# A transformer block with 32 routed experts: another order in the front, and a routing transition that keeps its second half off GpSimd

## The chip, the core and the metric

The kernel runs on one core of a Trainium2 chip. A core has five engines with a queue of instructions each: TensorE (PE; its weight loads are listed as PEld), VectorE (DVE), ScalarE (ACT), GpSimd (POOL) and SyncE (SP, which here only issues DMA transfers). An engine runs its queue in order; semaphores make an instruction wait for those of other engines. The metric is device time in microseconds, the median of several runs; chances further down are meant against the median before.

## What is computed

One layer on x (1024 tokens of 1024 numbers), float32, cut to what matters:

```python
c_act = silu(c)
sh1, sc1, gt1, sh2, sc2, gt2 = split(c_act @ w_ada + b_ada, 6)
h = rms_norm(x, g_mix) * (1 + sc1) + sh1
q_lat, kv_lat, k_rope, q_b, k_b, v_b, gate_a, gate_b = split(h @ w_in)
x = x + gt1 * (sigmoid(gate_a) * (mla(...) @ w_oa) + sigmoid(gate_b) * (band(...) @ w_ob)) @ w_out
h = rms_norm(x, g_ffn) * (1 + sc2) + sh2
group = top 1 of softmax(h @ w_rg + b_rg)               # 4 groups
two experts = top 2 of softmax((h @ w_re + b_re)[group]) # 8 in each group
x = x + gt2 * sum over the two of weight * (silu(h @ w_gate[e]) * (h @ w_up[e])) @ w_down[e]
return rms_norm(x, g_final)
```

## The kernel before

The program is recorded through a scheduler, which fixes each engine's order when it is built; `tc.issue_after(i)` tells it not to place instructions before i. Tiles come from shared pools of fixed places: `t8` (8 KB a partition, 18 places), `t4` (4 KB, 10) and `t2` (6). A transfer into a place waits until its former tile has been read for the last time. Products need more than one rounded factor: a float32 operand is split into a high part (ScalarE, L67 or L380) and a rest (VectorE, L68 or L381), and one product becomes three TensorE instructions (L72 to L74).

**The front** (`front`, L301). x comes in eight tiles of 128 tokens, four to a half, with the modulation weights `wada` (eight of 1 MB) and the latent weights `wl` (two of 832 KB). SP issues the first half of x, wada 0, wl 0, wada 1, the second half of x, wada 2, wl 1 (L324 to L333). For each half, `normal` (L345) squares the four tiles on ScalarE into one scratch place `junk` (L349), takes the reciprocal root in eleven small VectorE steps (L82 to L91) and scales the tiles (L352). `turn` (L357) transposes them, 32 TensorE instructions a half (L361), and ScalarE copies the result to `xT` (L362). `shift_scale(k)` (L367) makes the 128 shifts and 128 scales of block k of eight by two sums over a wada tile on VectorE (L371), `modulate` (L375) applies them on ScalarE (L378) and splits the result. `latent(h, k, pl)` adds the block's 12 products for half h. For the first four blocks the halves go apart (`APART = 4`), after that together. Values (L72 with `wvh`) follow directly; behind them come projections and attention to about 868 us.

**The merge and the routing** (`merge` L1000, `route` L1147, the class at L1547). Eight tiles of tokens get their output projection (L72 to L74 into `pp`), `gt1` times it (L1568, `part`), the sum with x (L1569), a sum of squares on ScalarE (L1577), the reciprocal root, and then the second modulation: a VectorE step x·rstd·a2 (L1594) and a GpSimd addition of sh2 (L1595), whose result is stored for the experts to gather. Logits come from x before its modulation (L1614; the scale is folded into `wr`), and `route(first, n)` takes them for four, two and two tiles: logits times rstd plus bias (L1157, L1158), the two largest of each group (L931 to L941), a mask of chosen experts `M` (L1177, L1178), running counts on TensorE (L1184, L1185), each token's place (`A`, L1212), and with these the list of tokens of each expert `idx` (L1238) and the weights `comb` (L1252). After the last call GpSimd gathers the tokens of expert 0 (L1341) and TensorE transposes them (L1492).

**The experts** (`weights`, L1277). 96 weights of 1 MB flow through a ring: the first 17 have places of their own (`RAW + RAW4`), 15 as one tile and two as pairs of 512 KB; later ones go round 14 whole places (`RAW2`) and the two pairs. From the fourth on a load waits for the last but one (L1299).

Of the kernel before, what the change touches and what calls it, by code (L numbers as in the profile page):

```python
# [19 lines left out]
P = 128  # L20
# [39 lines left out]
class Kernel:  # L60
# [240 lines left out]
    def front(self, c):  # L301
# [33 lines left out]
        load_mod(0)  # L335
        load_lat(0)
        load_mod(1)
        load_x(1)
# [5 lines left out]

        def normal(h):  # L345
            hs = slice(4 * h, 4 * h + 4)
            for t in range(4 * h, 4 * h + 4):
                junk = self.t4([P, D], F32, "junk")
                nc.scalar.activation(junk, xs[t], AF.Square, accum_out=ss[:, t:t + 1])  # L349
# [7 lines left out]
        def turn(h):  # L357
            for k in range(KD):
# [8 lines left out]
        def shift_scale(k):  # L367

            w = mods.pop(k)
            for i, (to, b) in enumerate(((shc, 19), (scc, 27))):  # L370
                nc.vector.tensor_tensor_reduce(w[:, i], w[:, i], cb, op0=OP.mult, op1=OP.add, scale=0.5,  # L371
                                               scalar=cols[:, b + k:b + k + 1], accum_out=to[:, k:k + 1])
            nc.vector.tensor_scalar(scc[:, k:k + 1], scc[:, k:k + 1], 1.0, cols[:, 8 + k:9 + k], op0=OP.add, op1=OP.mult)

        def modulate(k, *halves):  # L375
            cs = slice(halves[0] * HALF, (halves[-1] + 1) * HALF)
            y = self.H(xt, k)[:, cs]
            last = nc.scalar.activation(y, y, AF.Identity, bias=shc[:, k:k + 1], scale=scc[:, k:k + 1])  # L378
            hi = self.H(hh, k)[:, cs]
# [3 lines left out]
        hh, hl = ([self.t8([P, 2, S], F32R, nm) for _ in range(4)] for nm in ("hh", "hl"))  # L383
        self.hh, self.hl = hh, hl
        lat = [self.t8([P, 4, LAT], F32, "lat") for _ in range(2)]
# [9 lines left out]
        def keep(pl, h):  # L395
            for t in range(4):
                nc.scalar.copy(lat[h][:, t], pl[t])
# [47 lines left out]
        rooted = normal(0)  # L445
        turn(0)
# [3 lines left out]

        def begin(k):
            load_mod(k + 3)
            shift_scale(k)
            self.split(wlh[k // 4][:, k % 4], wll[k // 4][:, k % 4], wl[k // 4][:, k % 4])
        for k in range(APART):
            with tc.issue_after(rooted.ins):
                begin(k)
            parted[k] = modulate(k, 0)[1]
            latent(0, k, pl)
            if k == 1:  # L460
                rooted = normal(1)
                turn(1)
        nxt += [self.bank()[:, 0:LAT] for _ in range(4)]
        for k in range(APART):
            modulate(k, 1)
            latent(1, k, nxt)
        for k in range(APART, KD):
            with tc.issue_after(parted[max(k - 3, 0)].ins):
                begin(k)
# [453 lines left out]
    def first_max(self, rw, src, rows, n, name):  # L923

        nc = self.nc

        def wide(t):
            return t.rearrange("p (a o) -> p a o", o=1).to_broadcast([P, rows, n])
        iom = self.iom[:, 0:n].rearrange("p (o e) -> p o e", o=1).to_broadcast([P, rows, n])
        m = rw.tile([P, rows], F32, name=name + "m")  # L930
        nc.vector.tensor_reduce(m, src, op=OP.max, axis=AX.X)  # L931
        yield
        t = rw.tile([P, rows, n], F32, name=name + "t")
# [4 lines left out]
        f = rw.tile([P, rows], F32, name=name + "f")  # L938
# [61 lines left out]
    def merge(self):  # L1000
# [43 lines left out]
        self.X = [self.t4([P, D], F32, "X") for _ in range(2)]  # L1044
# [4 lines left out]
        for u in range(4):  # L1049
            steps = second.project(u, 1)  # L1050
            for _ in range(TURN_AT):
                next(steps)
            if u > 0:
                turn(second, u - 1)
            next(route, None)
            if u == 2:
                most = self.route(4, 2)
                next(most)
            elif u == 3:
                next(most)  # L1060
# [11 lines left out]
        next(most)  # L1072
        route = self.route(6, 2)
# [3 lines left out]
        stored = second.modulate(3)  # L1077
# [69 lines left out]
    def route(self, first, n):  # L1147
# [4 lines left out]
        lg = rw.tile([P, n, 4], F32, name="lg" + tag)  # L1152
        le = rw.tile([P, 4 * n, 8], F32, name="le" + tag)
        u = self.rstd[:, hs].rearrange("p (a o) -> p a o", o=1)
        for to, cs in ((le.rearrange("p (a g) e -> p a (g e)", a=n), slice(4, 36)), (lg, slice(0, 4))):
            w = cs.stop - cs.start
            nc.vector.tensor_mul(to, self.logits[first - base][:, base:base + n, cs], u.to_broadcast([P, n, w]))  # L1157
            nc.vector.tensor_add(to, to, self.rbias[:, cs].rearrange("p (o e) -> p o e", o=1).to_broadcast([P, n, w]))  # L1158
        found = {}

        def groups():
            found["g"] = yield from self.first_max(rw, lg, n, 4, "g" + tag)

        def tops():
            found["a"] = yield from self.first_max(rw, le, 4 * n, 8, "a" + tag)
# [3 lines left out]
            found["b"] = yield from self.first_max(rw, le, 4 * n, 8, "b" + tag)  # L1169
# [4 lines left out]
        mine = goh.rearrange("p a (g o) -> p (a g) o", o=1).to_broadcast([P, 4 * n, 8])  # L1174
        M = rw.tile([P, n, E], BF16, name="M" + tag)
        flat = M.rearrange("p a (g e) -> p (a g) e", g=4)
# [10 lines left out]
        for j, o in enumerate((oh1, oh2)):  # L1187
            nc.vector.tensor_mul(oh[:, :, j].rearrange("p a (g e) -> p a g e", g=4),
                                 o.rearrange("p (a g) e -> p a g e", a=n),
                                 goh.rearrange("p a (g o) -> p a g o", o=1).to_broadcast([P, n, 4, 8]))  # L1190
# [7 lines left out]
        nc.gpsimd.tensor_mul(m2, m2, goh.rearrange("p a g -> p (a g)"))  # L1198
        nc.vector.tensor_reduce(d[:, :, 4], m2.rearrange("p (a g) -> p a g", a=n), op=OP.add, axis=AX.X)
# [24 lines left out]
        C = self.t2([P, 2 * n, 3, E], BF16, "C")  # L1224
        nc.gpsimd.tensor_mul(C, oh8.rearrange("p n (o e) -> p n o e", o=1).to_broadcast([P, 2 * n, 3, E]),
                             parts.rearrange("p n (c o) -> p n c o", o=1).to_broadcast([P, 2 * n, 3, E]))
# [12 lines left out]
        yield  # L1239
        for i in range(N):  # L1240
# [36 lines left out]
    def weights(self, n):  # L1277

        for _ in range(n):
# [6 lines left out]
            elif j < RAW + RAW4:  # L1286
                w = [self.t4([P, D], F32, "we4") if j == RAW or c == 0 else self.more.tile([P, D], F32, name="we_more")
# [47 lines left out]

    def experts(self):
# [3 lines left out]
        def gather(e):  # L1340
            nc.gpsimd.indirect_dma_start(  # L1341
                out=X[e % 2], out_offset=None, in_=self.scratch["h2"],
                in_offset=bass.IndirectOffsetOnAxis(ap=self.idx[:, e:e + 1], axis=0),
                bounds_check=S - 1, oob_is_err=False)
# [4 lines left out]
        gather(0)  # L1349
        gather(1)  # L1350
        self.weights(RAW4 - 1)
# [192 lines left out]
class Mix:  # L1544
# [27 lines left out]
    def square(self, u, cs):  # L1572
# [4 lines left out]
        k.nc.scalar.activation(self.h2[u][:, cs], self.x1[u][:, cs], AF.Square, accum_out=ss)  # L1577
# [11 lines left out]
    def modulate(self, u):  # L1589
# [4 lines left out]
        nc.vector.scalar_tensor_tensor(h2, self.x1[u], k.rstd[:, t:t + 1], k.a2, op0=OP.mult, op1=OP.mult)  # L1594
        nc.gpsimd.tensor_add(h2, h2, k.sh2)  # L1595
# [26 lines left out]
def lay_out(i):  # L1622
# [6 lines left out]
    def col(v):  # L1629
# [16 lines left out]
        "w_mod": f["w_ada"][0][:, 0:2 * D].T.reshape(2, KD, P, D).transpose(1, 2, 0, 3),  # L1646
# [19 lines left out]
    }  # L1666
    return {k: np.ascontiguousarray(v) for k, v in out.items()}
# [16 lines left out]
```

## Time and profile before

| | us |
|---|---|
| median of 3 runs | 1294.43 |
| lowest, highest | 1293.18, 1301.65 |
| profiled execution | 1290.75 |
| its span | 1289.0 |
| PE busy | 1170.5 (91%) |
| DVE busy | 846.8 (66%) |
| ACT busy | 647.2 (50%) |
| POOL busy | 375.8 (29%) |

The profile is of one execution. Its span runs from the first to the last record; 1.75 us lie around it. Busy shares are means over stages that differ: TensorE works nearly without a break in most of the span, and stands for longer stretches in the first 45 us, around the routing at 870 to 906 us, and after 1244 us.

### The profile page before, as it was taken

Reading aid. Unit: us, or ns where it says so; the run is one execution under the profiler, and the core shown is the slowest. Engines: PE = TensorE matmul, PEld = TensorE weight load, DVE = VectorE, ACT = ScalarE, POOL = GpSimd, SP = SyncE. Lnnn points to the kernel's source line nnn. Section 1 sums busy time; section 2 is a strip of 40 time slices with the busy share of each in tenths; the row PEclk is TensorE's granted clock in tenths of the full one; section 3 lists DMA queues with packets and bytes.
Section 4 is the critical chain, followed back from the end, with each engine's and each line's share of the span. In section 5 each row is a group of like instructions: output and inputs, shape, how many; then the busy total and the mean of one; then the engine's idle time right before and its main releaser. Section 6 shows DMA issues by size and latency. Waiting matters only on the chain.

```text
span 1289.0 us, 17451 instructions
## 1 busy us (share of the span) xinstructions
PE 1170.5 (91%) x5802; PEld 941.2 (73%) x5802; DVE 846.8 (66%) x1709; ACT 647.2 (50%) x1277; POOL 375.8 (29%) x429
## 2 busy tenths in 40 slices
PE   3899989999999999999799999995899999998970
PEld 2887878788888888888688888874677667665640
DVE  6864636766766444677798826658777778666644
ACT  5563443544545445556678713212656656554522
POOL 0010322322322222233346465324223223232210
PEclk8999999999999999999899999996899999999985
DMA  9325885355453344797755455966788899989957
GB/s 377 133 95 190 249 262 177 112 166 186 127 183 112 99 135 140 265 317 230 210 182 161 160 201 172 366 246 244 243 289 287 294 312 295 311 308 299 313 172 272
DMA packets 102612, 286.50 MB, mean 222 GB/s; under 512 B 16453, under 2 KB 35013, under 8 KB 88344
## 3 DMA queue, kind: packets, MB, share of 16 engines
q1 hardware_dynamic: 84600, 242.34, 54.6%
q0 software_dynamic: 10864, 26.24, 8.1%
q10 hardware_dynamic: 7056, 16.78, 3.6%
q8 instruction: 47, 0.77, 0.2%
q14 instruction: 45, 0.37, 0.1%
HBM read 233.90 MB, written 68.17 MB: 234 GB/s over the span
## 4 chain that ended last, share of the span: by engine, by line
PE 59%; DMA 23%; DVE 9%; ACT 5%; issue 3%; POOL 1%; SPq 0%; DVEq 0%; POOLq 0%; ACTq 0%
DMA scratch_x<-eo,idx 11%; PE bank L72 9%; PE bank L74 9%; PE bank L73 9%; PE pp L74 4%; PE pp L72 4%; PE pp L73 4%; PE pp L1537 4%; DMA X<-scratch_h,idx 3%; PE bank L573 3%; PE bank L585 2%; PE bank L584 2%; DMA w<-in_w_g 2%; DMA scratch_oa<-ohl 2%; PE pp L1492 1%
## 5 line engine op out<-in xcount | busy, mean ns | idle before, releaser
L68 DVE TENSOR_TENSOR whl<-we,whl 128x1024 fp32r<-128x1024 f32 x125 | 150.3, 1221 | 52.4 <-ACT whl L67 49.2
L67 ACT CAST whl<-we 128x1024 fp32r<-128x1024 f32 x125 | 129.3, 1054 | 71.3 <-PE pp L74 55.3
L558 POOL TENSOR_SCALAR pr<-pr,total 128x640 f32<-128x640 f32 (+7 forms) x128 | 96.5, 756 | 209.3 <-DVE total L557 174.0
L72 PE MATMUL bank<-hh,wx 128*128 128x512 f32 x384 | 154.6, 402 | 1.4 <-DVE pl L68 1.4
L73 PE MATMUL bank<-hl,wx 128*128 128x512 f32 x384 | 151.4, 394 | 0.0
L74 PE MATMUL bank<-hh,wx 128*128 128x512 f32 x384 | 151.2, 395 | 0.0
L556 ACT ACTIVATE pr<-st,lowest 128x640 f32<-128x640 f32 (+7 forms) x128 | 89.7, 702 | 68.5 <-DVE lowest L549 43.1
L1398 POOL DMA_INDIRECT scratch_x<-eo,idx x32 | 55.9, 1747 | 229.0 <-DMA scratch_x<-eo,idx 87.8
L1537 PE MATMUL pp<-we,hT 128*128 128x512 f32 x248 | 115.6, 608 | 3.6 <-DMA we<-in_w_e 2.7
L72 PE MATMUL pp<-whl,xh 128*128 128x512 f32 x256 | 112.9, 441 | 3.5 <-ACT whl L67 3.4
L73 PE MATMUL pp<-whl,xh 128*128 128x512 f32 x256 | 104.4, 408 | 3.2 <-DVE whl L68 3.2
L68 DVE TENSOR_TENSOR pl<-bank,ph 128x512 fp32r<-128x512 f32 (+1 forms) x152 | 91.0, 612 | 23.0 <-ACT ph L67 21.1
L74 PE MATMUL pp<-whl,xl 128*128 128x512 f32 x256 | 101.4, 396 | 0.0
L592 POOL TENSOR_TENSOR ohl<-o,ohl 64x256 fp32r<-64x256 f32 x64 | 52.0, 813 | 138.2 <-ACT ohl L591 95.6
L67 ACT CAST ph<-bank 128x512 fp32r<-128x512 f32 (+1 forms) x152 | 77.6, 530 | 27.4 <-PE bank L573 25.4
L573 PE MATMUL bank<-ident,pr 128*128 128x128 f32 x528 | 81.8, 276 | 6.8 <-DVE st L553 6.7
L1537 PEld LDWEIGHTS pp<-we,hT 128*128 128x128 f32 x248 | 47.0, 194 | 52.0 <-issue 44.0
L72 PEld LDWEIGHTS bank<-hh,wx 128*128 128x128 f32 x384 | 72.7, 189 | 16.7 <-issue 2.6
L74 PEld LDWEIGHTS bank<-hh,wx 128*128 128x128 f32 x384 | 72.6, 189 | 15.3
L73 PEld LDWEIGHTS bank<-hl,wx 128*128 128x128 f32 x384 | 72.6, 189 | 12.4
L573 PEld LDWEIGHTS bank<-ident,pr 128*128 128x128 f32 x528 | 60.8, 141 | 12.7 <-issue 6.9
L73 PEld LDWEIGHTS pp<-whl,xh 128*128 128x128 f32 x256 | 48.7, 190 | 20.7 <-DVE whl L68 8.1
(375 smaller groups left out, 2820.3 us busy)
## 6 DMA issues: line engine op xcount, KB each, us to landing
we<-in_w_e SPq DMA_DIRECT2D x85, 1024.0 KB
mw<-in_w_ada SPq DMA_DIRECT2D x64, 256.0 KB
we<-in_w_e SPq DMA_DIRECT2D x17, 512.0 KB
x<-in_x SPq DMA_DIRECT2D x16, 512.0 KB
wada<-in_w_mod SPq DMA_DIRECT2D x8, 1024.0 KB
w<-in_w_g SPq DMA_DIRECT2D x16, 512.0 KB
scratch_gate<-gs ACTq DMA_DIRECT2D x32, 256.0 KB
gt<-scratch_gate SPq DMA_DIRECT2D x32, 256.0 KB
```

The costliest lines, as they stand in the source:

```text
L67: nc.scalar.copy(hi, src)
L68: (eng or nc.vector).tensor_sub(lo, src, hi.bitcast(F32))
L72: mm(ps, lh, rh, start=start, stop=False)
L73: mm(ps, lh, rl, start=False, stop=False)
L74: mm(ps, ll, rh, start=False, stop=stop)
L556: nc.scalar.activation(pv, sv, AF.Exp, bias=lowest, scale=-1.0, accum_out=total)
L558: nc.gpsimd.tensor_scalar(pr[:, 0:w], pr[:, 0:w], total, 1.0, op0=OP.mult, op1=OP.mult)
L573: nc.tensor.transpose(tp[:, i * P:(i + 1) * P], probs[s][:, lc:lc + P], self.ident)
L584: nc.tensor.matmul(o, vt[:, kb], pt["h"][:, src:src + n * P], start=i == 0, stop=False)
L592: nc.gpsimd.tensor_sub(hl[rows, 1], o[rows], hl[rows, 0].bitcast(F32))
L1398: self.nc.gpsimd.indirect_dma_start(out=self.scratch["x1"], out_offset=bass.IndirectOffsetOnAxis(ap=rows, axis=0), in_=o, in_offset=None, ...
L1537: nc.tensor.matmul(po[n], hT[:, ks], w[:, ns], start=k == 0, stop=k == 1)
```

## The change

In the front:

- x's second half is loaded right behind wada 0, ahead of wl 0 and wada 1.
- The squares (`sums`) of tiles 1 and 3 of the first half are made on VectorE (`SQUARES`), the others on ScalarE as before; all still write the one free `junk` place.
- For block 0 (`DIRECT = 1`) the scale comes from eight TensorE products with one column (L381 of the changed file) and one addition, in place of one of the two VectorE sums; the host lays out that part of wada 0 for it.
- The first transposes of half 0 are followed by its first modulation, and the other transposes come after; the second half's squares, scaling and transposes follow directly on block 0's products. `APART` is 2.

At the routing:

- For the second half of the tiles x·a2 is multiplied on VectorE right at the square (which now writes a scratch tile), and one VectorE step multiplies by rstd and adds sh2; GpSimd's addition is gone there.
- The logits of a tile are scaled and get their bias in one VectorE step a tile.
- The recorded order of `merge` differs: the last tile's modulation and store come ahead of the third call of `route`; the gathers of experts 0 and 1 are recorded before the last part of `route`; the product `C` is placed later.
- The ring: `RAW` 14, `RAW2` 13, `RAW4` 3, so three of the 16 round places are pairs; X takes one t8 tile. `LATE` is 3.

```diff
-LATE = 4
+LATE = 3
-APART = 4
+APART, DIRECT, SQUARES = 2, 1, ((1, 3), ())
-SPLIT, RAW, RAW2, RAW4 = 4, 15, 14, 2
+SPLIT, RAW, RAW2, RAW4 = 4, 14, 13, 3
         load_x(0)
         load_mod(0)
+        load_x(1)
         load_lat(0)
         load_mod(1)
-        load_x(1)
...
+        def sums(h):
+            for t in range(4 * h, 4 * h + 4):
+                junk = self.t4([P, D], F32, "junk")
+                if t % 4 in SQUARES[h]:
+                    nc.vector.tensor_tensor_reduce(junk, xs[t], xs[t], op0=OP.mult, op1=OP.add, scale=1.0, scalar=0.0,
+                                                   accum_out=ss[:, t:t + 1])
+                else:
+                    nc.scalar.activation(junk, xs[t], AF.Square, accum_out=ss[:, t:t + 1])
...
+            if k < DIRECT:
+                wk = w[:, 1].rearrange("p (b c) -> p b c", b=KD)
+                pc = self.bank()
+                for r in range(KD):
+                    nc.tensor.matmul(pc[:, 0:1], wk[:, r], cact[:, r:r + 1], start=r == 0, stop=r == KD - 1)
+                nc.vector.tensor_add(scc[:, k:k + 1], pc[:, 0:1], cols[:, 27 + k:28 + k])
...
-        rooted = normal(0)
-        turn(0)
+        sums(0)
+        normal(0)
+        weights(0)
+        turn(0, range(1))
+        modulate(0, 0)
+        turn(0, range(1, KD))
...
             latent(0, k, pl)
-            if k == 1:
+            if k == 0:
+                sums(1)
                 rooted = normal(1)
                 turn(1)
...
-        for to, cs in ((le.rearrange("p (a g) e -> p a (g e)", a=n), slice(4, 36)), (lg, slice(0, 4))):
-            w = cs.stop - cs.start
-            nc.vector.tensor_mul(to, self.logits[first - base][:, base:base + n, cs], u.to_broadcast([P, n, w]))
-            nc.vector.tensor_add(to, to, self.rbias[:, cs].rearrange("p (o e) -> p o e", o=1).to_broadcast([P, n, w]))
+        for i in range(n):
+            nc.vector.scalar_tensor_tensor(lr[:, i], self.logits[first - base][:, base + i], self.rstd[:, first + i:first + i + 1],
+                                           self.rbias, op0=OP.mult, op1=OP.add)
...
+        if self.half:
+            k.nc.vector.tensor_mul(self.h2[u][:, cs], self.x1[u][:, cs], k.a2[:, cs])
...
-        nc.vector.scalar_tensor_tensor(h2, self.x1[u], k.rstd[:, t:t + 1], k.a2, op0=OP.mult, op1=OP.mult)
-        nc.gpsimd.tensor_add(h2, h2, k.sh2)
+        if self.half:
+            nc.vector.scalar_tensor_tensor(h2, h2, k.rstd[:, t:t + 1], k.sh2, op0=OP.mult, op1=OP.add)
+        else:
+            nc.vector.scalar_tensor_tensor(h2, self.x1[u], k.rstd[:, t:t + 1], k.a2, op0=OP.mult, op1=OP.mult)
+            nc.gpsimd.tensor_add(h2, h2, k.sh2)
```

What this makes of the engines' queues is seen at three places. Line numbers in a row are those of the file that it comes from. First TensorE's queue where the second half's transposes (L361, in the changed file L367) stand against the first latent products (`st<-wlh,hh`: half 0; `bank<-wlh,hh`: half 1); before:

```order
L73 MATMUL st<-wll,hh 128x416
L74 MATMUL st<-wlh,hl 128x416
L361 MATMUL bank<-ident,x 128x128 x32
L72 MATMUL bank<-wlh,hh 128x416
L73 MATMUL bank<-wll,hh 128x416
```

and now:

```order
L381 MATMUL bank<-cact,wada 128x1 x8
L367 MATMUL bank<-ident,x 128x128 x41
L72 MATMUL st<-wlh,hh 128x416 x2
L367 MATMUL bank<-ident,x 128x128 x19
L73 MATMUL st<-wll,hh 128x416
L74 MATMUL st<-wlh,hl 128x416
L72 MATMUL st<-wlh,hh 128x416
```

All 64 transposes but four now stand ahead of the third latent product; before, 24 products of half 0 stood between the two halves' transposes.

Second, ScalarE's queue from the squares to the first modulation (L378, now L392); before:

```order
L349 ACTIVATE junk,ss<-x 128x1024 x4
L362 COPY xT<-bank 128x512 x2
L349 ACTIVATE junk,ss<-x 128x1024
L362 COPY xT<-bank 128x512 x3
L349 ACTIVATE junk,ss<-x 128x1024
L362 COPY xT<-bank 128x512 x2
L67 CAST wlh<-wl 128x416 x2
L349 ACTIVATE junk,ss<-x 128x1024
L67 CAST wlh<-wl 128x416 x2
L362 COPY xT<-bank 128x512
L378 ACTIVATE xT<-xT,shc,scc 128x512 x2
L349 ACTIVATE junk,ss<-x 128x1024
```

and now:

```order
L352 ACTIVATE junk,ss<-x 128x1024
L317 ACTIVATE cb<-st 128x1024
L352 ACTIVATE junk,ss<-x 128x1024 x5
L368 COPY xT<-bank 128x512 x2
L392 ACTIVATE xT<-xT,shc,scc 128x512
L397 CAST hh<-xT 128x512
L368 COPY xT<-bank 128x512 x5
L67 CAST wlh<-wl 128x416 x4
L368 COPY xT<-bank 128x512 x4
```

The second half's four squares stood between copies, casts and modulations; now all of them come before the first copy.

Third, VectorE's queue at the routing, where the last tile's `part` and sum with x stand against the second call of `route` (names with 0; `M_8919` is its mask); before:

```order
L1178 TENSOR_TENSOR M_8919<-M_8919,g0t 128x64
L1208 RECIPROCAL den_9007<-den_9007 128x4
L1181 TENSOR_TENSOR before<-before,M_8919 128x32
L1210 SCALAR_TENSOR_TENSOR vals<-den_9007 128x2
L1181 TENSOR_TENSOR before<-before,M_8919 128x32
L1202 TENSOR_TENSOR slot_at<-oh,pp 128x128
L1206 TENSOR_REDUCE place<-slot_at 128x4
L1212 TENSOR_TENSOR A<-io,place 128x512
L1568 TENSOR_TENSOR part<-pp,gt_7757 128x512
L1569 TENSOR_TENSOR x_8484<-x_8484,part 128x512
```

and now:

```order
L966 TENSOR_TENSOR b0t<-lr_8891,b0m 128x64
L968 TENSOR_TENSOR b0t<-b0t,iom 128x64
L1606 TENSOR_TENSOR part<-pp,gt_7760 128x512
L971 TENSOR_REDUCE b0f<-b0t 128x8
L1233 TENSOR_REDUCE d_9066<-b0m 128x2
L1607 TENSOR_TENSOR x_8487<-x_8487,part 128x512
L973 TENSOR_TENSOR b0t<-iom,b0f 128x64
L1238 TENSOR_REDUCE den_9074<-d_9066 128x2
L1241 TENSOR_SCALAR den_9074<-d_9066 128x2
L1618 TENSOR_TENSOR h_8999<-x_8487,a_7862 128x512
L1212 TENSOR_TENSOR M_8919<-a0t,b0t 128x64
L1223 TENSOR_TENSOR oh<-b0t,g0t 128x2x32
```

The last tile's sum with x moved from behind the whole second call to the middle of it, ahead of its mask, and the two kinds of work now alternate.

## Rows read from the trace of the kernel before

**Rows 1.** Stretches: length; PE, PEld, DVE, ACT, POOL busy (instructions); PE's clock; DMA; GB/s
```profile
0.00:30.30 30.30, 10.58 (x36) 6.98 (x36) 18.63 (x69) 18.82 (x35) 0.70 (x6) 0.91 0.93 375
30.30:44.70 14.40, 10.82 (x57) 9.87 (x57) 13.80 (x33) 6.47 (x13) 0.00 (x0) 0.83 0.50 208
44.70:78.00 33.30, 33.30 (x169) 32.86 (x169) 18.54 (x30) 19.14 (x28) 0.00 (x0) 0.95 0.20 64
78.00:868.00 790.00, 764.00 (x4083) 646.44 (x4082) 497.77 (x1120) 391.33 (x885) 265.11 (x332) 0.99 0.59 193
882.90:905.90 23.00, 8.02 (x44) 6.48 (x44) 20.00 (x61) 6.60 (x11) 12.72 (x24) 0.50 0.47 156
```
**Rows 2.** ScalarE's order of time, 6 to 38 us: start, duration, line, operation, idle before
```profile
18.48 1.07 ACT L362 COPY xT<-bank 128x512 f32<-128x512 f32 x2 [6.15 <-PE bank L361]
28.59 1.09 ACT L349 ACTIVATE junk<-x 128x1024 f32<-128x1024 f32 x1
```
**Rows 3.** VectorE's order of time, 6 to 38 us
```profile
12.35 0.17 DVE L82 TENSOR_SCALAR rs_v<-ss 128x4 f32<-128x4 f32 x1 [1.69 <-ACT junk L349]
14.53 2.74 DVE L352 TENSOR_SCALAR x<-x,rstd 128x1024 f32<-128x1024 f32 x4
17.19 1.28 DVE L371 CUSTOM_DVE_ANT_0 wada<-wada,cb,cols 128x1024 f32<-128x1024 f32 x1
24.52 1.09 DVE L68 TENSOR_TENSOR wll<-wl,wlh 128x416 fp32r<-128x416 f32 x2 [2.17 <-ACT wlh L67]
32.96 2.74 DVE L352 TENSOR_SCALAR x<-x,rstd 128x1024 f32<-128x1024 f32 x4
```
**Rows 4.** TensorE's order of time, 0 to 45 us
```profile
15.43 6.91 PE L361 MATMUL bank<-ident,x 128*128 128x128 f32 x32 [8.75 <-DVE x L352]
30.33 0.72 PE L72 MATMUL st<-wlh,hh 128*128 128x416 f32 x1 [7.99 <-ACT hh L380]
36.91 0.35 PE L74 MATMUL st<-wlh,hl 128*128 128x416 f32 x1
37.10 1.91 PE L361 MATMUL bank<-ident,x 128*128 128x128 f32 x16
44.68 0.46 PE L72 MATMUL bank<-wlh,hh 128*128 128x416 f32 x1 [3.20 <-ACT hh L380]
```
**Rows 5.** Shorter stretches of TensorE alone: us, PE busy (x), PEclk, DMA share, GB/s
```profile
15.40:17.10 1.70, 1.67 (x8) 1.00 0.99 395
21.40:22.20 0.80, 0.80 (x8) 1.00 0.96 399
30.30:35.10 4.80, 4.77 (x14) 0.50 1.00 416
```
**Rows 6.** VectorE's order of time at the routing, 868 to 906 us
```profile
876.95 2.33 DVE L1158 TENSOR_TENSOR lg<-lg,rbias 128x8 f32<-128x8 f32 x1
...
885.40 0.68 DVE L1568 TENSOR_TENSOR part<-pp,gt 128x512 f32<-128x512 f32 x1
886.12 0.69 DVE L1569 TENSOR_TENSOR x<-x,part 128x512 f32<-128x512 f32 x1
...
891.13 2.38 DVE L1158 TENSOR_TENSOR le<-le,rbias 128x64 f32<-128x64 f32 x1
893.44 0.15 DVE L1158 TENSOR_TENSOR lg<-lg,rbias 128x8 f32<-128x8 f32 x1
893.55 0.22 DVE L931 TENSOR_REDUCE a2m<-le 128x8 f32<-128x64 f32 x1
...
899.84 0.80 DVE L1238 TENSOR_TENSOR idx<-slot_acc 128x32 int32<-128x32 f32 x1
```
**Rows 7.** GpSimd's order of time there
```profile
891.10 2.34 POOL L1595 TENSOR_TENSOR h<-h,sh 128x1024 f32<-128x1024 f32 x1 [4.93 <-ACT whl L67]
```
**Rows 8.** TensorE's order of time there: the last tile's last projection product; expert 0
```profile
877.45 0.40 PE L74 MATMUL pp<-woh,m 128*128 128x512 f32 x1
...
905.92 1.30 PE L1492 MATMUL pp<-ident,X 128*128 128x128 f32 x5 [4.80 <-DMA X<-scratch_h,idx]
```
**Rows 9.** SP's waits, 905 to 1260 us: total, times, longest
```profile
SPq L1299 <- DMA we<-in_w_e: 251.9, 68, 8.6
SPq L1299 <- DMA we_more<-in_w_e: 18.2, 5, 5.9
SPq L1299 <- DVE comb L1252: 11.8, 1, 11.8
```

More of the change, by code (lines that the diff above doesn't have):

```diff
@@ L355, in front, with turn @@
         xt = [self.t8([P, 2, S], F32, "xT") for _ in range(4)]
-        def turn(h):
-            for k in range(KD):
+        def turn(h, ks=range(KD)):
+            for k in ks:
                 pt = self.bank()
@@ L381, in modulate @@
             return last, nc.vector.tensor_sub(self.H(hl, k)[:, cs], y, hi.bitcast(F32))
-        hh, hl = ([self.t8([P, 2, S], F32R, nm) for _ in range(4)] for nm in ("hh", "hl"))
+        hh, hl = [], []
         self.hh, self.hl = hh, hl
-        lat = [self.t8([P, 4, LAT], F32, "lat") for _ in range(2)]
+        lat = {}
         ssl = one.tile([P, NT, 2], F32, name="ssl")
@@ L449, in front @@
         nxt, parted = [], {}
[L451 to L454, printed above, removed]
         for k in range(APART):
-            with tc.issue_after(rooted.ins):
-                begin(k)
-            parted[k] = modulate(k, 0)[1]
+            if k > 0:
+                weights(k)
+            if k > 0:
+                modulate(k, 0)
+            split_lat(k)
             latent(0, k, pl)
-            if k == 1:
+            if k == 0:
+                sums(1)
                 rooted = normal(1)
@@ L464, in front @@
         for k in range(APART):
-            modulate(k, 1)
+            parted[k] = modulate(k, 1)[1]
             latent(1, k, nxt)
         for k in range(APART, KD):
-            with tc.issue_after(parted[max(k - 3, 0)].ins):
-                begin(k)
+            with tc.issue_after(parted[k - 3].ins if k > 2 else rooted.ins):
+                weights(k)
+                split_lat(k)
             last, parted[k] = modulate(k, 0, 1)
@@ L937, in first_max @@
         yield
-        f = rw.tile([P, rows], F32, name=name + "f")
+        f = rw.tile([P] + rows, F32, name=name + "f")
         nc.vector.tensor_reduce(f, t, op=OP.min, axis=AX.X)
@@ L1043, in merge @@
         project(second, 3, 0)
-        self.X = [self.t4([P, D], F32, "X") for _ in range(2)]
+        both = self.t8([P, 2, D], F32, "X")
+        self.X = [both[:, i] for i in range(2)]
         for x in self.X:
@@ L1072, in merge @@
         next(most)
+        next(most)
+        stored = second.modulate(3)
         route = self.route(6, 2)
@@ L1076, in merge @@
             pass
-        stored = second.modulate(3)
+        next(route)
+        next(route)
+        for e in range(2):
+            self.gather(e)
         for _ in route:
@@ L1168, in tops @@
             yield
-            found["b"] = yield from self.first_max(rw, le, 4 * n, 8, "b" + tag)
+            found["b"] = yield from self.first_max(rw, le, [n, 4], 8, "b" + tag)
         chains = [tops(), groups()]
@@ L1239, in route @@
         yield
+        C = self.t2([P, 2 * n, 3, E], BF16, "C")
+        with ExitStack() as c:
+            if first == 6:
+                c.enter_context(self.tc.issue_after(self.routed.ins))
+            nc.gpsimd.tensor_mul(C, oh8.rearrange("p n (o e) -> p n o e", o=1).to_broadcast([P, 2 * n, 3, E]),
+                                 parts.rearrange("p n (c o) -> p n c o", o=1).to_broadcast([P, 2 * n, 3, E]))
         for i in range(N):
@@ L1286, in weights @@
             elif j < RAW + RAW4:
-                w = [self.t4([P, D], F32, "we4") if j == RAW or c == 0 else self.more.tile([P, D], F32, name="we_more")
+                w = [self.t4([P, D], F32, "we4") if j < RAW + RAW4 - 1 or c == 0 else self.more.tile([P, D], F32, name="we_more")
                      for c in range(2)]
@@ L1334, in halves, with gather @@
         return wh, wl
+    def gather(self, e):
+        self.nc.gpsimd.indirect_dma_start(
+            out=self.X[e % 2], out_offset=None, in_=self.scratch["h2"],
+            in_offset=bass.IndirectOffsetOnAxis(ap=self.idx[:, e:e + 1], axis=0),
+            bounds_check=S - 1, oob_is_err=False)
     def experts(self):
@@ L1338, in experts @@
         X = self.X
[L1340 to L1344, printed above, removed]
+        gather = self.gather
         def scatter(e, o):
             self.add_rows(o, self.idx[:, e:e + 1])
-        gather(0)
-        gather(1)
-        self.weights(RAW4 - 1)
+        self.weights(RAW + RAW4 - len(self.loads))
         self.xT = [self.t4([P, KD, P], F32R, nm) for nm in ("xh", "xl")]
@@ L1576, in square @@
         ss = k.small.tile([P, 1], F32, name="ss%d" % cs.start)
-        k.nc.scalar.activation(self.h2[u][:, cs], self.x1[u][:, cs], AF.Square, accum_out=ss)
+        out = k.t2([P, D], BF16, "squares") if self.half else self.h2[u]
+        k.nc.scalar.activation(out[:, cs], self.x1[u][:, cs], AF.Square, accum_out=ss)
+        if self.half:
+            k.nc.vector.tensor_mul(self.h2[u][:, cs], self.x1[u][:, cs], k.a2[:, cs])
         return ss
@@ L1645, in lay_out @@
         "c_row": f["c"].reshape(1, D),
-        "w_mod": f["w_ada"][0][:, 0:2 * D].T.reshape(2, KD, P, D).transpose(1, 2, 0, 3),
+        "w_mod": f["w_ada"][0][:, 0:2 * D].T.reshape(2, KD, P, D).transpose(1, 2, 0, 3).copy(),
         "w_ada": f["w_ada"][0][:, 2 * D:],
@@ L1666, in lay_out @@
     }
+    out["w_mod"][0:DIRECT, :, 1] = (f["w_ada"][0][:, D:2 * D].reshape(KD, P, KD, P)
+                                    .transpose(2, 1, 0, 3).reshape(KD, P, D)[0:DIRECT])
     return {k: np.ascontiguousarray(v) for k, v in out.items()}
```

54 lines of the change are left out of this document (30 added, 24 removed).

## The prediction

> **What bounds the kernel now.** I began with a table of stretches. From 78 to 868 us TensorE is busy 764.0 of 790 us, and from 44.7 to 78.0 all 33.3 [rows 1]. Nothing the change touches lies there, and a packed stretch keeps its length when it starts earlier. What can be won is idle TensorE time: 19.7 us in the first 30.3, 3.6 in the next 14.4, 15.0 of the 23 us around the routing [rows 1]. So I read the order of time of TensorE in these stretches, then of the engines it waits for.
>
> In the front TensorE transposes at 15.43, then waits 8.0 us for `hh`, makes 24 products, transposes the second half at 37.10 and waits 3.2 us again before 44.68 [rows 4]. The second half is late because its squares stand between copies on ScalarE: the last begins at 28.59 [rows 2], the reciprocal root and the scaling (2.74 from 32.96) follow [rows 3]. At the routing the last projection product ends at 877.85 [rows 8], but `part` reads it at 885.40 [rows 6]: VectorE has the whole second call of `route` ahead of it. Twice a tiny addition there takes 2.3 to 2.4 us, where another of its kind takes 0.15 [rows 6]; the second runs with GpSimd's addition of sh2 from 891.10 to 893.44 [rows 7]. Expert 0 waits for `idx` and its gather until 905.92 [rows 6, 8]. Last I read SP's waits: after the routing it waits mostly for weights, and once, 11.8 us, for `comb`, the routing's last result [rows 9].
>
> **The front, step by step.** Moving x ahead of 1.9 MB: x, wada 0 and nothing else are 5.2 MB, 14 us at the 375 GB/s of the first 30 us [rows 1], a mean that includes the empty start; I take 14 to 17 us for x's last tile. With no copies between them, the second half's squares (1.09 each) end about 1.2 us later, at 18; before, the last ended at 29.7 [rows 2]. VectorE's two squares in the first half win little: all write one `junk`, so they run one after the other. VectorE pays: one shift sum of 1.28 now stands among the root's steps of the first half, and rope steps (an estimate of 0.3) too, so scaling starts at 16.1, not 14.53 [rows 3]. One of the two sums of block 0 goes (1.28); eight one-column products and one addition replace it, and their cost I take as nothing, because TensorE stands idle ahead of its first transpose (8.75 us) [rows 4]. Without that cover, eight products at most as long as a transpose at 0.2 [rows 5] cost 1.6.
>
> VectorE then goes: scaling to 18.8; the second root, 2.2 (12.35 to 14.53); the rest of `hh`, 0.7; scaling, 2.74; two sums, 2.5; three rests of `wl`, 0.55 each [rows 3]. That ends at 28.6. ScalarE, from its first copy at 19.3 (0.8 later than 18.48), has 16 copies of 0.53 [rows 2], one modulation and cast (about 1.2) and four casts (about 1.8): all done near 31. TensorE's 64 transposes are paced by these copies; the products proper start at about 29.5, before 30.33, but now with the second half transposed too, except four.
>
> From there: 192 latent products at the 0.19 spacing of 36.91 to 37.10 [rows 4], 0.187 by 12 in a row, are 35.9 us; four transposes 0.5; waits for the second half's `hh` and for block 1's, which ScalarE delivers one modulation and one cast at a time from 31 on, about 3.4. 29.5 + 35.9 + 0.5 + 3.4 = 69.3, against 78.0 [rows 1]: **8.7 us** won. With no wait at all it would be 65.9 (12.1 won). Behind this the engine is packed, so the shift carries on to 868.
>
> A clock question decides the lower end. Of the granted clock the trace shows 0.50, the 1.2 GHz level, in the first products: 14 in 4.8 us, 0.34 each, after an idle stretch of 8 us [rows 4, 5]. In the transposes ahead of that the column shows 1.00, yet eight took 1.7 us at first and eight took 0.8 six microseconds later [rows 5]. Their pace doubled with nothing but transposes on the engine, so I let transposes bring back the 2.4 GHz level, and price all products by the short spacing. The Trainium skill, "TensorE: Matmul & The Clock Gate", Part 4: PE-mode transpose, speaks against this change: transposes don't count as busy time, and full clock doesn't engage for them. By the rule the 60 transposes ahead would not warm the engine, and the sum would be that of the late clock below; the trace's halved spacing disagrees with it.
>
> **The routing, step by step.** The last tile's `part` can't start before 877.85 [rows 8]. In the new order it stands behind the third tile's second modulation step (1.28), half of the last tile's x·a2 (0.65) and some fifteen small steps; I count the sum with x done at 880.2, where it was 886.8 [rows 6]: 6.6 earlier. From there to `a2m` it was 6.7 us (886.8 to 893.55) [rows 6]. Of this 2.2 goes (the addition held beside GpSimd, 2.38 against 0.15) [rows 6, 7]; what alternates with the root's steps now, the mask, the counts and `A`, adds about 2.5. The x·a2 product and the step with sh2 are 1.28 each where there was one such step; the product lies beside the square on ScalarE and costs 0.65 for its late half at most, in the 2.5. `a2m` comes at about 887.3: **6.3 us** won. From `a2m` to `idx` (6.3 us) and to expert 0 nothing is changed: `C` still stands ahead of the gather in GpSimd's queue. Bounds: all of the delay from 877.85 to 885.40 and no more, 7.6; only the two held additions, 4.4. The first modulation's store comes earlier with it, the gathers' recording moves no queue. SP's next load waited for `comb` and moves along [rows 9].
>
> **The ring.** The third pair makes one load in 16 two transfers; its cost I take as nothing: SP waits 3.6 us a load for pair halves (18.2 over 5) and 3.7 for whole loads (251.9 over 68) [rows 9]. X in one larger place and `LATE` shift no load behind another that is waited for.
>
> **Sum.** 8.7 + 6.3 = 15.0. The profiled execution's 1290.75 would be 1275.8. It lies 3.7 below the median of 1294.43, so by the median: **1279.4**.
>
> **Rivals.**
> - *The stream stays put.* If the experts' end hangs on the weights, and the first load after the routing waits for another place than that of `comb`, the routing's 6.3 is given back before the end. For it: SP's 252 us of waits for weights; against: the 11.8 us for `comb` [rows 9]. 1294.4 - 8.7 = 1285.7.
> - *Late clock.* Transposes spread thin by the copies leave the clock low: 14 products at 0.34 for 0.19 are 2.2, eight transposes at 0.21 for 0.10 another 0.9 [rows 5]. For it: the low clock after every gap so far; against: transposes at double pace. 1294.4 - 5.6 - 6.3 = 1282.5.
> - *The front does not get shorter.* The order on one `junk` keeps the squares apart, and ScalarE's copies, not the squares, are what TensorE waits for. Against: four squares leave the copies' stretch. 1294.4 - 6.3 = 1288.1.
> - *Everything shorter.* No wait in the latents, and all of the routing's delay: 1294.4 - 12.1 - 7.6 = 1274.7.
> - *Slower: the pairs thin the stream.* 79 loads go round 16 places, so the third pair is loaded about six times. If each such load costs the difference between the longest wait, 8.6, and the mean, 3.7 [rows 9], that is 4.9 × 6 = 29.4: 1308.8. It turns the change slower than before from 2.5 us a load. Against it: the equal mean waits.
>
> **How the numbers follow.** A measurement of this kernel tells about 1% (12.9 us, so 1281.5 and 1307.4) from no change. Chances: forecast 0.56, stream 0.12, late clock 0.10, everything shorter 0.10, front not shorter 0.07, slower 0.05. The forecast's own range is 1275 to 1284 (waits in the front ±3, routing 4.4 to 7.6); four fifths of it, 0.45, lie below 1281.5. Faster by over 1%: 0.45 + 0.10 = 0.55. Within 1%: 0.11 + 0.12 + 0.10 + 0.07 = 0.40. Slower: 0.05. The range 1273 to 1288 leaves out the slower case, most of the front that does not shorten and the end of the shorter one, some 0.15.
>
> **What would show it.** Right: transposes of both halves end by 31, the first latent products of half 1 start near 33, the first value product (L72, `wvh`) near 69; products at 0.19 from the start; `a2m` 6 us nearer to the last projection product, no addition at the routing over 1 us, `comb` and the next load 15 us earlier, and the same 15 at the end. Wrong: a granted clock of 0.50 under the products at 30; `part` still waiting for `A`; a gap in TensorE among the experts where a pair lands.

## The result, and the profile after

The changed kernel takes 1278.11 us (median of 4 runs, 1272.52 to 1280.87); beside it the kernel before took 1295.20. The ratio is 0.9864 (0.9824 to 0.9904). In a second set, beside the variants below, the ratio was 0.9856 (0.9788 to 0.9924). Forecast were 1279.4 us and a gain of 15.0; measured is 17.1. The profiled execution took 1279.66 (before 1290.75), its span is 1277.9. So the two profiles lie 11.1 us apart, not 17.1: the one before was 4.5 us below its median, the one after 1.6 above. What follows accounts for the 11.1.

First the table of stretches of the kernel after, cut at its own stages: the start of the products, and the ends of the latents, of attention, of the last projection product, of the wait for expert 0 and of the last down product (the experts' last). Columns are as in [rows 1]:

```profile
0.00:27.40 27.40, 17.82 (x81) 13.36 (x82) 23.32 (x84) 18.30 (x33) 0.70 (x6) 1.00 0.92 366
27.40:65.50 38.10, 37.21 (x198) 35.92 (x196) 27.65 (x48) 23.82 (x33) 0.00 (x0) 1.00 0.44 169
65.50:751.40 685.90, 656.71 (x3517) 555.87 (x3515) 436.78 (x962) 367.59 (x819) 219.31 (x288) 0.99 0.57 180
751.40:870.70 119.30, 119.29 (x627) 100.84 (x627) 72.14 (x190) 28.64 (x75) 44.92 (x47) 1.00 0.73 258
870.70:891.50 20.80, 7.02 (x57) 5.63 (x55) 19.20 (x69) 5.61 (x9) 10.75 (x24) 0.60 0.83 314
891.50:1244.40 352.90, 332.69 (x1346) 228.87 (x1346) 250.54 (x318) 192.36 (x286) 90.65 (x61) 0.98 0.86 284
```

The kernel before, cut at the same stages behind the latents, which end at 78.0:

```profile
78.00:756.90 678.90, 654.48 (x3518) 554.78 (x3516) 436.90 (x962) 367.23 (x819) 220.13 (x289) 0.99 0.57 182
756.90:877.80 120.90, 119.31 (x622) 100.11 (x623) 68.46 (x173) 27.41 (x72) 48.32 (x46) 1.00 0.72 261
877.80:905.90 28.10, 9.81 (x61) 8.14 (x60) 24.84 (x86) 6.81 (x12) 15.10 (x28) 0.57 0.56 199
905.90:1255.50 349.60, 332.12 (x1346) 228.51 (x1346) 249.84 (x318) 192.14 (x286) 90.00 (x61) 0.98 0.86 287
```

Read them in pairs. The latents end 12.5 us earlier. Attention, the same instructions, is 7.0 longer (685.9 against 678.9), the merge 1.6 shorter, the way from the last projection product to expert 0 7.3 shorter, the experts 3.3 longer: 12.5 - 7.0 + 1.6 + 7.3 - 3.3 = 11.1, the difference of the spans. TensorE's busy time hardly moves (1170.5 before, 1170.8 after); what changes is its idle time.

TensorE's order of time in the front, kernel after, beside [rows 4]:

```profile
11.96 3.54 PE L381 MATMUL bank<-cact,wada 128*128 128x1 f32 x16 [5.42 <-DVE rs_i L83]
15.98 6.69 PE L367 MATMUL bank<-ident,x 128*128 128x128 f32 x33 [0.48 <-DVE x L358]
22.83 1.31 PE L367 MATMUL bank<-ident,x 128*128 128x128 f32 x8 [0.15 <-ACT xT L368]
23.90 0.63 PE L72 MATMUL st<-wlh,hh 128*128 128x416 f32 x2
...
25.56 2.12 PE L367 MATMUL bank<-ident,x 128*128 128x128 f32 x16 [0.71 <-ACT xT L368]
27.44 0.44 PE L73 MATMUL st<-wll,hh 128*128 128x416 f32 x1
...
30.19 0.45 PE L72 MATMUL bank<-wlh,hh 128*128 128x416 f32 x1 [0.19 <-ACT hh L397]
...
34.44 0.46 PE L72 MATMUL bank<-wlh,hh 128*128 128x416 f32 x1 [0.63 <-ACT hh L397]
```

The waits of 8.0 and 3.2 us before have become 0.19 and 0.63. The granted clock reads 1.00 all the way, but that is not TensorE's pace at the start: the first transposes stand 0.21 us apart, as before (eight in 1.70 us from 15.98), and only from about 21 us on are they at 0.11 (eight in 0.90 us from 21.80). The products behind them keep the short spacing of 0.19. VectorE's two scalings and ScalarE's last square:

```profile
15.08 2.74 DVE L358 TENSOR_SCALAR x<-x,rstd 128x1024 f32<-128x1024 f32 x4
...
21.47 2.73 DVE L358 TENSOR_SCALAR x<-x,rstd 128x1024 f32<-128x1024 f32 x4
```

```profile
17.02 1.06 ACT L352 ACTIVATE junk<-x 128x1024 f32<-128x1024 f32 x1
```

The second half is scaled 11.5 us earlier than at 32.96 [rows 3]. VectorE at the routing, with TensorE's last projection product and its first transposes of expert 0, beside [rows 6, 8]:

```profile
870.78 0.69 DVE L1606 TENSOR_TENSOR part<-pp,gt 128x512 f32<-128x512 f32 x1 [0.36 <-POOL b0m L1232]
...
878.83 0.22 DVE L963 TENSOR_REDUCE a2m<-lr 128x8 f32<-128x64 f32 x1
...
885.13 0.81 DVE L1269 TENSOR_TENSOR idx<-slot_acc 128x32 int32<-128x32 f32 x1
```

```profile
870.28 0.39 PE L74 MATMUL pp<-woh,m 128*128 128x512 f32 x1
...
891.48 1.94 PE L1530 MATMUL pp<-ident,X 128*128 128x128 f32 x8 [5.06 <-DMA X<-scratch_h,idx]
```

`part` starts 0.1 us behind the product that it reads, where it started 7.6 us behind it before.

### The profile page after: what moved, and what is told of

It reads as the page before. It is cut to its first block, busy times and chain, and to the rows that moved or that the text cites. A ratio compares the mean times of both kernels' runs of the same rounds, so it can differ in the third digit from the quotient of the medians.

```text
span 1277.9 us, 17482 instructions
## 1 busy us (share of the span) xinstructions
PE 1170.8 (92%) x5818; PEld 940.5 (74%) x5818; DVE 845.5 (66%) x1711; ACT 645.5 (51%) x1269; POOL 367.9 (29%) x425
## 4 chain that ended last, share of the span: by engine, by line
PE 60%; DMA 24%; DVE 9%; issue 3%; ACT 3%; POOL 1%; SPq 0%; DVEq 0%; POOLq 0%; ACTq 0%
DMA scratch_x<-eo,idx 12%; PE bank L72 9%; PE bank L73 9%; PE bank L74 8%; PE pp L72 5%; PE pp L74 5%; PE pp L73 5%; PE pp L1575 4%; PE bank L600 3%; DMA X<-scratch_h,idx 2%; PE bank L612 2%; PE bank L611 2%; DMA w<-in_w_g 2%; DMA mw<-in_w_ada 1%; PE pp L1530 1%
## 5 line engine op out<-in xcount | busy, mean ns | idle before, releaser
L1575 PE MATMUL pp<-we,hT 128*128 128x512 f32 x248 | 112.1, 593 | 2.0 <-DMA we<-in_w_e 1.2
L68 DVE TENSOR_TENSOR pl<-bank,ph 128x512 fp32r<-128x512 f32 (+1 forms) x152 | 91.1, 613 | 22.7 <-ACT ph L67 20.7
L74 PEld LDWEIGHTS bank<-hh,wx 128*128 128x128 f32 x384 | 72.4, 189 | 15.3
```

What stands on the lines that cost most here:

```text
L68: (eng or nc.vector).tensor_sub(lo, src, hi.bitcast(F32))
L74: mm(ps, ll, rh, start=False, stop=stop)
L1575: nc.tensor.matmul(po[n], hT[:, ks], w[:, ns], start=k == 0, stop=k == 1)
```

## The experiments

All variants are of the changed kernel, but for E1, E2 and E10. Stage times are of one profiled execution each; *attention* is from the first value product to the first output projection product, *idx* (its end) and *expert 0* (its first transpose) are counted from the end of the last projection product. The kernel before, run beside each set, had means of 1295.7 to 1296.8 us. Two means of ten to sixteen runs each leave some 3.5 to 4.5 us open between them, worked out from the scatter of the runs.

| | runs | mean us | ratio (interval) | first value product | attention | idx | expert 0 |
|---|---|---|---|---|---|---|---|
| before | | | 1 | 77.97 | 678.9 | 22.8 | 28.1 |
| after | 4 | 1277.4 | 0.9864 (0.9824 to 0.9904) | 65.48 | 685.9 | 15.3 | 20.8 |
| E1 front only | 12 | 1285.4 | 0.9921 (0.9887 to 0.9956) | 65.66 | 683.3 | 22.8 | 28.1 |
| E2 routing only | 12 | 1287.2 | 0.9914 (0.9884 to 0.9945) | 78.66 | 682.3 | 15.3 | 21.8 |
| E3 x late | 10 | 1289.3 | 0.9955 (0.9920 to 0.9989) | 78.76 | 679.7 | 15.3 | 20.8 |
| E4 squares on ScalarE | 4 | 1275.7 | 0.9844 (0.9783 to 0.9904) | 65.05 | 685.1 | 15.3 | 20.7 |
| E5 after again | 4 | 1275.6 | 0.9856 (0.9788 to 0.9924) | 65.51 | 683.2 | 15.3 | 21.9 |
| E6 GpSimd adds | 4 | 1273.2 | 0.9844 (0.9769 to 0.9918) | 65.72 | 679.0 | 18.5 | 24.0 |
| E7 old order | 4 | 1275.9 | 0.9853 (0.9782 to 0.9925) | 65.53 | 686.4 | 17.1 | 22.4 |
| E8 old ring | 10 | 1283.9 | 0.9908 (0.9872 to 0.9943) | 65.49 | 685.8 | 15.3 | 20.6 |
| E9 both old | 4 | 1277.7 | 0.9839 (0.9768 to 0.9911) | 65.54 | 683.9 | 20.0 | 25.4 |
| E10 before, warm | 10 | 1291.7 | 0.9965 (0.9929 to 1.0001) | 76.12 | 679.8 | 22.8 | 28.3 |
| E11 three loads | 4 | 1282.0 | 0.9871 (0.9799 to 0.9942) | 65.51 | 686.6 | 15.3 | 20.8 |
| E12 old ring, LATE 3 | 6 | 1282.0 | 0.9871 (0.9821 to 0.9920) | 65.69 | 685.7 | 15.5 | 21.0 |

**E1, E2: the change in two.** E1 takes the hunks of `front` alone, E2 all others.

> The front as changed, the routing and the ring as before. In the changed kernel the first value product came at 65.5 us, 12.5 earlier than before, but only 6.3 of it were left when the merge began. Theory A (attention gives it back: a fixed part of the front's gain is lost to waits for ScalarE and VectorE and to short drops of the granted clock behind 80 us): first value product at 65 to 66, shift 5 to 8 us at the merge, time 5 to 8 us below the kernel before. Theory B (that loss is the scatter of one execution): the shift at the merge is above 9 us, time 9 to 12 us below.

> The routing, its recorded order and the ring as changed, the front as before. Theory A (the routing wins about 8 us and the weight stream takes some of it back behind 1160 us): a2m comes about 8 us nearer to the last projection product of the kernel before, time 5 to 8 us below. Rival (the stream sets the end wherever the routing ends): the same at a2m, time within 2 us of the kernel before.

The front's 12.3 us at the latents are there in E1. For the rest the test is split: the one profile has a shift of 7.9 us left at the merge, which is theory A's, while the mean time fell by 11.4 us, which is theory B's. E2's routing is 7.5 us shorter at `idx`, and its mean fell by 9.6 us, above theory A's 5 to 8 though not beyond the scatter. E2 also holds the new ring, which E8 and E12 take out.

**E3: x's second half late.**

```diff
-        load_x(1)
         load_lat(0)
         load_mod(1)
+        load_x(1)
```

> The changed kernel with x's second half loaded in its old place, behind wl 0 and wada 1. Theory A (the early load is what lets the second half's squares go ahead of the copies): the last square ends 4 to 5 us later, near 23, the first value product 2 to 5 us later, 67.5 to 70.5. Rival (TensorE waits for ScalarE's copies and the rests of wl, not for x): first value product within 1 us of 65.5.

Theory A is right in direction and far off in size. The last square of the second half ends at 25.9 us, not near 23 (18.2 in the changed kernel), and the first value product comes 13.3 us later: more than the whole front had won. TensorE's order of time in E3:

```profile
30.73 5.78 PE L367 MATMUL bank<-ident,x 128*128 128x128 f32 x32
...
54.52 0.46 PE L72 MATMUL st<-wlh,hh 128*128 128x416 f32 x1 [4.48 <-ACT hh L397]
```

All 32 transposes of the second half now stand behind block 0's first two products, from 30.73 on, and the other products start at 36.3, where it was 27.4; then a new wait for `hh` of 4.5 us follows. A likely reason for it, not tested, is that with `APART` 2 there are fewer products of half 0 to lie beside the second half's copies and modulations. The ten runs lie 13 us above the twelve of the changed kernel, E4 and E5, and no lower than E2 with the whole old front: the new order pays only with the early load. (In the one profile E3's first product also came 1.5 us later than in the changed kernel, at 4.26, and the first half's transposes 2.3 later, at 18.32, so a part of the 13.3 may be the scatter of one execution.)

**E4: all squares on ScalarE** (`SQUARES = ((), ())`).

> The changed kernel with all squares on ScalarE, as before. Theory A (one scratch place keeps the squares one after the other, so VectorE's two win next to nothing): first value product within 0.7 us of 65.5. Rival (they save two squares of ScalarE's time at the start, 2.3 us, and cost VectorE nothing): scaling of the first half and the first value product 1 to 2.3 us later.

Theory A: the first value product came 0.4 us earlier than after, the scaling at 14.47 instead of 15.08. VectorE's squares are no visible part of the front's gain.

**E5 to E7, E9: what shortens the routing.** E6 puts back the VectorE step with rstd and a2 and GpSimd's addition of sh2:

```diff
-        if self.half:
-            k.nc.vector.tensor_mul(self.h2[u][:, cs], self.x1[u][:, cs], k.a2[:, cs])
...
-        if self.half:
-            nc.vector.scalar_tensor_tensor(h2, h2, k.rstd[:, t:t + 1], k.sh2, op0=OP.mult, op1=OP.add)
+        nc.vector.scalar_tensor_tensor(h2, self.x1[u], k.rstd[:, t:t + 1], k.a2, op0=OP.mult, op1=OP.mult)
+        nc.gpsimd.tensor_add(h2, h2, k.sh2)
```

E7 puts back the recorded order of the second call of `route` and of the last tile's modulation (that of the gathers and of `C` stays new), E9 does both:

```diff
             elif u == 3:
+                next(most)
...
         next(most)
-        next(most)
-        stored = second.modulate(3)
         route = self.route(6, 2)
         next(route)
         for _ in most:
             pass
+        stored = second.modulate(3)
```

> The changed kernel once more, beside the variants of it that follow. Both theories: first value product at 65 to 66 us; from the last projection product to a2m 8.4 us, as in its first profile, where it was 16.1 before. Theory A (behind 80 us a fixed part of the front's gain is given back): shift against the kernel before 5 to 7 us when the merge begins. Theory B (scatter): another value, up to 10.

> The changed kernel, but with GpSimd adding sh2 for the second half too, as before (one VectorE step, one GpSimd step a tile); the new order stays. Theory A (the held additions were one cause, the order the other): logits' steps on VectorE take up to 2.4 us again beside GpSimd's addition, and from the last projection product to a2m it is 10.5 to 13 us. Rival (the order alone made the gain): 8 to 9 us.

> The changed kernel with the old recorded order of the second call of route and of the last tile's modulation; GpSimd stays out of the second half. Theory A: part waits for A again, but no addition is held: from the last projection product to a2m 11 to 13 us, so the order is worth 3 to 4 and the missing GpSimd step the rest of 7.7. Rival (GpSimd alone): 8 to 9 us.

> The changed kernel with both parts of the routing undone: the old recorded order, and GpSimd adding sh2; the one-step logits, the early record of the gathers and the ring stay. Alone, GpSimd's step took idx from 15.3 to 18.5 us behind the last projection product, the old order to 17.1; before it was 22.8. Theory A (the two add up, and the rest of the 7.5 is the one-step logits): about 20.3. Rival (the two lock into each other: the held addition delays what stands ahead of the last tile): 21.5 to 23.

E5, the changed kernel again, has 8.2 us left of the front's shift at the merge, where the first profile had 5.5: theory B, that number scatters. From the last projection product to `a2m` it was 8.2 us in E5, 9.5 in E6, 10.0 in E7, 11.2 in E9 (before 15.7). E6 and E7 lie just below theory A's ranges and above the rivals'; E9's `idx`, 20.0, is what the two add up to (15.3 + 3.2 + 1.8 = 20.3). The missing GpSimd step is worth 3.2 us at `idx`, the order 1.8, and the remaining 2.8 (22.8 - 20.0) goes with what E9 keeps: the one-step logits, perhaps, which no run took out alone. E6, VectorE and then GpSimd, with the same VectorE step in E7 between them:

```profile
875.25 0.22 DVE L963 TENSOR_REDUCE a2m<-lr 128x8 f32<-128x64 f32 x1
875.50 2.10 DVE L966 TENSOR_TENSOR a2t<-lr,a2m 128x64 f32<-128x64 f32 x1
```

```profile
881.35 0.22 DVE L966 TENSOR_TENSOR a2t<-lr,a2m 128x64 f32<-128x64 f32 x1
```

```profile
875.18 2.34 POOL L1634 TENSOR_TENSOR h<-h,sh 128x1024 f32<-128x1024 f32 x1 [1.47 <-DVE h L1633]
```

The hold has found another VectorE step with two SBUF inputs (SBUF is the memory that the tiles lie in): 2.10 us where the same step takes 0.22 in E7, till GpSimd is done. The reduction ahead of it, with one input, was not held. The held step stands behind `a2m`, which is why E6 falls short of theory A's range there (1.4 us later than E5) and shows its 3.2 only at `idx`. The Trainium skill, "SBUF — State Buffer", section "SBUF: two separate sides", states this: a VectorE instruction with two SBUF inputs and a GpSimd instruction that reads SBUF exclude each other, and the later one waits for the whole of the other. The rows agree.

**E8, E12: the ring.** E8 has the old ring (`RAW, RAW2, RAW4` 15, 14, 2), X as two t4 tiles and `LATE` 4; E12 the same with `LATE` 3.

> The changed kernel with the old ring (15 whole places and two pairs, 14 of them round), X as two smaller tiles, LATE 4. Theory A (the third pair costs nothing): TensorE waits among the experts for whl and for weights as long as in the changed kernel, some 14 us in sum by its profile, time within 3 us of it. Rival (the third pair is what makes weights late behind 1160 us): these waits fall to about 9 us as in the kernel before, time 4 to 6 us shorter.

> The changed kernel with the old ring and the two smaller X tiles, but LATE 3 as changed: of the kernel with the old ring it differs by the place of one early weight load alone. With the old ring and LATE 4 the ten runs had a mean of 1283.8 us; the changed kernel and its variants with the new ring lie at 1276 to 1278. Theory A (the ring and X are worth those 6 to 7 us): 1282 to 1286. Rival 1 (the early load ahead of the last store was what cost): 1275 to 1279. Rival 2 (the ring does nothing, and what ten runs showed was scatter): also 1275 to 1279, and then the two can't be told apart.

The sixteen runs of E8 and E12 have a mean of 1283.2, the twelve of the changed kernel, E5 and E4 one of 1276.3: 6.9 us, with an uncertainty of 3.4 from their scatter. So the ring (with X's place, which was not taken apart from it) is worth about 7 us, in time the largest part after the front. E12 by itself, at 1282.0, lies at the edge of theory A's range and 5.7 us above those twelve, but its interval overlaps with the changed kernel's, so the share of `LATE` stays open. Where these 7 us lie no profile shows: from expert 0 to the last down product it is 350.5 us in E8, 357.7 in E12, 352.9 in the changed kernel and 351.0 in E5. Among the experts TensorE waits 7.1 us for `whl` and weights in E8, 13.9 in the changed kernel, but 8.1 in E5, which is the same kernel: the rival's smaller waits are there, its shorter time is not, and theory A's equal time isn't either.

**E10: the clock.** Into the kernel before go 60 transposes behind `turn(0)` and 24 behind `turn(1)`.

```diff
+        def warm(n, x):
+            pt = self.bank()
+            for i in range(n):
+                nc.tensor.transpose(pt[:, 0:P], x[:, (i % KD) * P:(i % KD + 1) * P], self.ident)
+        warm(60, xs[3])
...
+                warm(24, xs[7])
```

> The kernel before with 60 more transposes, whose results nobody reads, between the first half's transposes and the first latent product, and 24 behind the second half's: TensorE is not idle there. They change nothing of the result. Theory A (transposes count for the clock, and the front's gain contains the low clock of 30 to 35 and 45 to 48 us): granted clock 1.00 from 22 to 50, products at 0.19 from the first, first value product 2.5 to 3.6 us earlier than 77.97. Rival (transposes do not bring the clock up or hold it): 0.50 under the first products as before, first value product not earlier than 77.5.

E10's TensorE alone in two stretches, columns as in [rows 5]:

```profile
22.40:30.30 7.90, 6.43 (x59) 1.00 1.01 419
30.30:35.10 4.80, 4.79 (x26) 1.00 1.02 423
```

The same 4.8 us that held 14 products at 0.50 [rows 5] hold 26 at 1.00. That is theory A on the clock. The first value product gained 1.9 us, below the 2.5 to 3.6; a likely reason is that the 24 transposes at the second place take until 43.4 us themselves. In time it is 0.9965 (0.9929 to 1.0001), so a gain in the whole is not shown.

**E11: three loads under way** (`DEPTH, THROTTLE = 3, 4`).

> The changed kernel with three weight loads under way where there were two (a load waits for the last but two). Theory A (the expert stage is paced by the weights, which take back part of an earlier routing): from expert 0's transposes to the last down product 340 us or less instead of 351 to 353, time 4 to 10 us below the changed kernel. Rival (the gathers, which wait behind the weights' transfers, get later instead): the same or longer, TensorE waiting for X.

Neither: behind expert 0 TensorE waits for no weight and no X, and the experts take 346.2 us to the last down product instead of 352.9, but from there to VectorE's last step it takes 40.3 us instead of 29.5, and the time is not shorter than after. The profile shows what the end then waits for: GpSimd issues the last scatter of the experts' results 11.6 us behind the last down product (1250.42), where it was 1.0 behind it, because each scatter waits for the one before. No variant beats the changed kernel beyond the intervals.

## Why the prediction was right, step by step

- **The front, 8.7 us: right in mechanism, undersized.** Scaling began at 15.08 (forecast 16.1), the last square of the second half ended at 18.2 (18), products from 27.4 (29.5), half 1 from 30.2 (33), and from there to the first value product TensorE was idle for 0.9 us (3.4 us of waits were set): 12.5, what "everything shorter" gave the front. The mis-sized terms are the start of the products, 2.1 us too late, and the waits, 2.5 too long. The eight products with one column took 3.54 us, not 1.6 at most, under the cover that was named: the first scaled tile came at 15.75.
- **The clock: right.** Products ran at 0.19 from the first; in E10 transposes alone hold the 2.4 GHz level from 22.4 to 30.3 us (59 in 6.43 us at 1.00). The rival "late clock", which had set 3.1 us for the opposite, is not what these runs show.
- **"The shift carries on to 868": wrong.** Of 12.5 us 5.5 were left at the merge. The step that failed is "the engine is packed": the stretch that was carried over unchanged holds 24 us of idle TensorE time before and 29 after. Over the ten profiles whose first value product comes early attention takes 684.5 us on average, over the four where it comes late (before, E2, E3, E10) 680.2: some 4 us are given back, and single executions with the early front range over 7.6. One place where executions differ is where TensorE waits for ScalarE's exponentials ahead of a band unit's products. Before, and in E6:

```profile
190.81 0.39 PE L784 MATMUL st<-kd,q 128*128 128x256 f32 x1 [3.76 <-ACT pr L556]
```

```profile
178.77 0.39 PE L811 MATMUL st<-kd,q 128*128 128x256 f32 x1 [1.74 <-ACT pr L583]
```

  The stretch around it in E6 (columns as in [rows 5]):

```profile
180.00:190.00 10.00, 10.00 (x47) 1.00 0.52 159
```

  And both in E7:

```profile
181.32 0.58 PE L811 MATMUL st<-kd,q 128*128 128x256 f32 x1 [5.21 <-ACT pr L583]
```

```profile
180.00:190.00 10.00, 8.68 (x27) 0.66 0.31 108
```

  After the wait of 1.7 us the clock stays at 1.00. After the 5.2 it has a mean of 0.66 in these ten us, whose first 1.3 are still the wait, and 47 instructions become 27. But this place explains only a part. The wait there is 4.5 to 5.9 us in seven of the ten profiles with the early front and 0.7 to 3.5 in three, against 3.4 to 4.4 in the four with the late one. If TensorE's 3517 instructions of this stage are matched one by one over the fourteen profiles, about 1 us of the 4 is lost around this place, and about 2.7 between 495 and 576 us behind the first value product. Why the early front loses time there is not settled.
- **The routing, 6.3 us: right in mechanism and a little undersized at `idx`, doubtful at the end.** At `a2m` 7.5 us were won, at expert 0 7.3; the merge was 1.6 shorter in this pair of profiles. But in time E1 (old routing, old ring, 1285.4) and the sixteen runs with new routing and old ring (1283.2) differ by 2.3, with 3.5 of uncertainty; and E6, E7 and E9, whose expert 0 comes 1.6 to 4.6 us later than after, are not slower. So most of the routing's gain seems to be lost among the experts, as in the rival "the stream stays put" (0.12), though 6.3 lies barely outside what the runs allow, and no profile shows the place.
- **The ring, 0: wrong.** It is worth about 7 us; the equal mean waits on SP, on which the zero rested, did not show it, and the cause is open. The slower rival, which made it a cost, had the wrong sign.
- **The sum.** In time the front brings about 11 (E1 against 1296.5 before, and E2 against the changed kernel), the routing about 2, the ring about 7, each with some 3.5 of uncertainty: 20, beside 15.0 forecast and 17.1 in the first comparison. Term by term that is some 2 above the forecast, 4 below and 7 above. That the total lay so near is in part luck: the routing's carry and the ring were wrong in opposite directions, and within the front the 3.8 us that were undersized stand against the 4 that attention took back.

## What to carry to other kernels

Price a term to the end of the program, not to the end of its stage: here a shift of 12.5 us was 8 on average one stage later, and 7.5 us at a routing step were about 2 in time (with 3.5 of uncertainty). A change that looks like bookkeeping (which places of a ring are whole and which are pairs, and where X lies) can be worth as much as the visible one; undo it by itself. And where only a few per cent move, one profile tells where a stage waits and a dozen runs tell the time: the one does not replace the other.

## What the hardware showed unexpectedly

- A held VectorE step is not a matter of which instruction it is: in E6, where the held additions of before are gone, the hold falls on the next step with two SBUF inputs (2.33 and 2.38 us before, 2.19 and 2.10 in E6, all beside a GpSimd addition of 2.34 to 2.40).
- Eight products with one column took 3.54 us, about as long as 16 transposes at the low pace [rows 5]: the trace lists 16 records for them.
- Transposes whose result nobody reads, put into an idle stretch, kept the granted clock at 1.00 where it had fallen to 0.50, and the first value product came 1.9 us earlier (E10).
